# Gate and up projections with the weights as the stationary operand, and small loads moved in the load queue

## The chip, the cores and the metric

The kernel runs on one core of a Trainium2 chip. TensorE (PE in the profile) multiplies 128x128 tiles: a weight load (PEld) puts the stationary operand into the array, then a matmul streams the moving operand past it, up to 512 columns, and adds into a bank of PSUM. VectorE (DVE), ScalarE (ACT) and GpSimd (POOL) do the elementwise work, and SyncE (SP) issues nearly all DMAs, each of which moves 512 KB of weights from memory into a buffer on the chip. Each engine takes its instructions in the order in which the program lists them, and waits on semaphores where it needs another engine's result. The metric is the device time of one execution in microseconds (us), the median of several.

## The reference, cut to what matters

Two layers, each with a half-step SwiGLU FFN, a block of three token mixers and a second FFN. There are 256 tokens, the model's width is 1024 and the FFN's is 2816; everything is float32.

```python
def swiglu_ffn(h, w_gate, w_up, w_down):
    return (jax.nn.silu(h @ w_gate) * (h @ w_up)) @ w_down

for l in range(DEPTH):                                   # DEPTH = 2
    x = x + 0.5 * swiglu_ffn(rms_norm(x, ffn1_norm[l]), ffn1_w_gate[l], ffn1_w_up[l], ffn1_w_down[l])
    h = rms_norm(x, mix_norm[l])
    p = h @ w_in[l]                                      # 2320 columns, then attention, gMLP, linear attention
    ...
    x = x + (mixed @ w_out[l]).astype(x.dtype)
    x = x + 0.5 * swiglu_ffn(rms_norm(x, ffn2_norm[l]), ffn2_w_gate[l], ffn2_w_up[l], ffn2_w_down[l])
```

## The kernel before

**Three products for one.** A float32 operand is split into a high part (rounded to float32r, which TensorE takes in one pass) and a low part (the rest). A product is then high x high, high x low and low x high: `mm3` issues these three matmuls, and each has a weight load of its own.

**Weights.** All weights come in units of 128 x 1024 (512 KB). `Unit.split` loads one into a ring of 4 raw buffers (`load`, L166), casts it to the high part on ACT (`act`, L140, 128x1024) and subtracts that on DVE for the low part (`vec`, L155, two of 128x512). The high and low parts have rings of 10 buffers each.

**FFN.** The hidden width is cut into NJ = 11 blocks `j` of 256 columns. For each of the two token tiles t (128 tokens), `gate_up(j, t)` takes the transposed, normalized activations `hT[t]` as stationary operand and streams 512 columns of weights, 256 of gate and 256 of up, over eight slices kc of the model's width: 8 x 3 = 24 matmuls of 512 columns into a bank `gu`. ACT takes the silu of the gate half (scaled by `rstd[t]`, a number per token, which is a partition here) and DVE multiplies it by the up half. The result has tokens on the partitions, so `turn_act(j)` transposes it with four PE transposes (L123) into a bank `tr` and splits it into high and low parts (ACT cast, DVE subtraction). `down(j, t)` then uses it as stationary operand against the down weights, 12 matmuls of 512 columns into the banks `acc`. A block has 2 x 24 + 2 x 12 = 72 such matmuls. The second tile's `down` of the last two blocks is held back for `finish_b`, so that the first tile's residual and norm overlap with matmuls.

**Mixers.** `mix_phase` has five projections with the same `mm3` (four of 512 columns, one of 272), attention scores with float32r matmuls of 256 columns, many small matmuls, and an output projection. Its small parameters `col`, `row`, `wg` and `wsT` are loaded by SP (L166); `kgain` is a product of two columns of `col` on DVE.

**Order.** Every operation is first recorded in a `Plan` with an estimated cost. `issue()` simulates the engines with these costs and writes each engine's list, always taking the ready operation with the longest path to the end; matmuls marked bulk keep their order among themselves and give way to the others. `after=` adds a dependency for this planning alone. A load that depends on nothing is planned as soon as the load queue is free.

Of the kernel before, what the change touches and what calls it, by code (L numbers as in the profile page):

```python
# [17 lines left out]
P = 128  # L18
D = 1024
KC = D // P  # L20
# [20 lines left out]
class Plan:  # L41
# [72 lines left out]

    def mm(self, out, lhsT, rhs, start=True, stop=True, bulk=False, shared=False):
        n = rhs.free_size()
        cost = n / 2400.0 + 0.003 if lhsT.dtype == F32R else 4 * n / 2400.0 + 0.005
        return self.add("PE", cost, lambda: self.nc.tensor.matmul(out, lhsT, rhs, start=start, stop=stop,  # L118
                                                                  skip_group_check=shared),
                        [out], [lhsT, rhs], bulk)  # L120
# [40 lines left out]
    def pool(self, cost, call, writes, reads=()):  # L161
        return self.add("POOL", cost, call, writes, reads)

    def load(self, out, in_):
        nbytes = out.free_size() * out.partition_size() * 4
        return self.add("DMA", max(0.1, nbytes / 360e3), lambda: self.nc.sync.dma_start(out=out, in_=in_), [out], [])  # L166

    def load_small(self, out, in_):
        return self.add("ACT", 0.1, lambda: self.nc.scalar.dma_start(out=out, in_=in_), [out], [])
# [50 lines left out]
def hybrid_trunk(ctx: ExitStack, tc: tile.TileContext, x_in, norms, w_gu1, w_d1, w_in, w_out,  # L220
# [19 lines left out]
    for name in ("acc0", "acc1", "acc2", "acc3", "gu0", "gu1", "tr0", "tr1"):  # L240
        banks[name] = ps.tile([P, 512], F32, tag=name, name=name)
        pl.psum.add(banks[name].tensor.name)
    turns = {"gu": 0, "tr": 0}

    def bank(kind):
        if kind in turns:
            turns[kind] ^= 1
            return banks[f"{kind}{turns[kind]}"]
        return banks[kind]
# [11 lines left out]
    tri, upp, bdm = tile_("tri", P), tile_("upp", P), tile_("bdm", P)  # L261
    gcol = tile_("gcol", 3 * L, KC)
    xt = [tile_(f"x{t}", D) for t in range(2)]
    hT = [[tile_(f"h{t}{i}", KC, P, dtype=F32R) for i in range(2)] for t in range(2)]
    mix_a = [tile_(f"ma{i}", 2, 4, P, dtype=F32R) for i in range(2)]
    mix_b = [cut(hT[1][i], "p (t c) q -> p t c q", t=2) for i in range(2)]
    q_hl = tile_("q_hl", 8, 2, 64, dtype=F32R)
# [5 lines left out]
    flat = cut(E[1], "p h k q -> p (h k q)")  # L273
    acts = [flat[:, i * FB:(i + 1) * FB] for i in range(4)]
    gates_ = [flat[:, (4 + i) * FB:(5 + i) * FB] for i in range(2)]
    hg = Ring("hg", 2, 4, P)
    junk = cut(E[0], "p h k q -> p (h k q)").bitcast(BF16)[:, 0:D]
    raws = Ring("raw", RAW_BUFS, UW)
# [62 lines left out]
    pl.pool(0.5, lambda: make_identity(nc, ident), [ident])  # L341
    pl.vec("tensor_copy", out=ident_r, in_=ident)
    fill(mhalf, -0.5)
    pl.load_small(gcol, norms)
    for t in range(2):
        for n in range(2):
# [2 lines left out]

    def constants():  # L350
        fill(lrT, 1.0)
        for t in (wg, v_pad, kst, attnT, amask, bdm):
            fill(t, 0.0)
        select(amask[:, 0, :], [[1, P]], 0, -1, ALU.is_gt, NEG)
        select(amask[:, 1, :], [[-1, P]], 0, 1, ALU.is_ge, NEG)
        fill(tri, 1.0 / 16.0)
        fill(tri[0:64, 64:128], 0.0)
        select(tri, [[1, P]], 0, -1, ALU.is_ge, 0.0)
        fill(upp, 1.0 / 16.0)
        fill(upp[64:128, 0:64], 0.0)  # L360
        select(upp, [[-1, P]], 0, 1, ALU.is_gt, 0.0)
        fill(bdm[0:64, 0:64], 1.0)
        fill(bdm[64:128, 64:128], 1.0)


    rstd = [None, None]
    last_silu = [None]

    def rsqrt_mean(name, n, ssum, scale):
        v = small("v" + name, n)  # L370
# [36 lines left out]
    def ffn_phase(l, gu, dn):  # L407
        acc = [[banks["acc0"], banks["acc1"]], [banks["acc2"], banks["acc3"]]]
        g_units = [units_of(gu[l, j], UW, 4) for j in range(NJ)]
        d_units = [units_of(dn[l, j], UW, 2) for j in range(NJ)]  # L410
        act_tiles = {}
        aT = [[cut(mix_a[i][:, s], "p (t f) q -> p t f q", t=2) for i in range(2)] for s in range(2)] + [a_third]

        def gate_up(j, t):
            o = bank("gu")
            hi, lo = hT[t]
            for kc in range(KC):
                u = g_units[j][kc // 2]
                s = slice((kc % 2) * 512, (kc % 2) * 512 + 512)
                mm3(o, hi[:, kc, :], lo[:, kc, :], u.h[:, s], u.l[:, s], kc == 0, kc == KC - 1)  # L420
            sg, a = gates_[t], acts[2 * (j % 2) + t]
            pl.act(sg, o[:, 0:FB], AF.Silu, scale=rstd[t], extra=1.283 if j == 0 and t == 0 else 0.0)
            last_silu[0] = pl.ops[-1]
            pl.vec("scalar_tensor_tensor", out=a, in0=o[:, FB:2 * FB], scalar=rstd[t], in1=sg,
                   op0=ALU.mult, op1=ALU.mult)
            act_tiles[j, t] = a

        def turn_act(j):
            tr = cut(bank("tr"), "p (t f q) -> p t f q", t=2, f=2)
            for t in range(2):  # L430
                for f in range(2):
                    pl.turn(tr[:, t, f, :], act_tiles[j, t][:, f * P:(f + 1) * P], ident)
            split_psum(aT[j % 3][0], aT[j % 3][1], tr)

        def down(j, t):
            hi, lo = aT[j % 3]
            for f, n in ((0, 0), (1, 0), (0, 1), (1, 1)):
                u = d_units[j][f]
                s = slice(n * 512, (n + 1) * 512)
                mm3(acc[t][n], hi[:, t, f, :], lo[:, t, f, :], u.h[:, s], u.l[:, s],  # L440
                    j == 0 and f == 0, j == NJ - 1 and f == 1)

        for j in range(NJ):
            ready(g_units[j])
            gate_up(j, 0)
            if j > 0:
                turn_act(j - 1)
            gate_up(j, 1)
            if j > 0:
                ready(d_units[j - 1])  # L450
                down(j - 1, 0)
                if j < NJ - 2:
                    down(j - 1, 1)
                elif j == NJ - 1:
                    down(j - 2, 1)
        turn_act(NJ - 1)
        ready(d_units[NJ - 1])

        def finish_a():
            down(NJ - 1, 0)  # L460
            return acc[0]

        def finish_b():
            down(NJ - 2, 1)
            down(NJ - 1, 1)
            return acc[1]

        return finish_a, finish_b, 0.5


    def mix_phase(l):
        pl.load(col, pcol[l])
        pl.load(row, prow[l].partition_broadcast(P))
        pl.vec("tensor_tensor", out=kgain, in0=col[:, 0:1], in1=col[:, 1:2], op=ALU.mult)
        pl.load(wg[0:17], gla_wg[l])
        pl.load(wsT, sgu_wT[l])
        select(wsT, [[0, 4], [1, P]], 0, -1, ALU.is_ge, 0.0)

        off, i_units = 0, []
# [322 lines left out]
def _layout(inp):  # L802
    import numpy as np

    a = {k: np.ascontiguousarray(v) for k, v in inp.items()}

    def tiles(w):
        return np.ascontiguousarray(w)

    def gate_up(g, u):  # L810
        gu = np.stack([g.reshape(L, KC, P, NJ, FB), u.reshape(L, KC, P, NJ, FB)], axis=4)
        return tiles(gu.transpose(0, 3, 2, 1, 4, 5)).reshape(L, NJ, P, KC * 2 * FB)

    def down(w):
        return tiles(w.reshape(L, NJ, 2, P, D).transpose(0, 1, 3, 2, 4)).reshape(L, NJ, P, 2 * D)

    w = a["w_in"]
    aq = w[:, :, 0:512].reshape(L, D, 2, 4, 64).transpose(0, 1, 3, 2, 4).reshape(L, D, 512)
    kvl = np.concatenate([w[:, :, 512:768], w[:, :, 2304:2320]], axis=2)
    groups = [aq, kvl, w[:, :, 1280:1792], w[:, :, 1792:2304], w[:, :, 768:1280]]  # L820
    w_in = np.concatenate(
        [g.reshape(L, KC, P, g.shape[2]).transpose(0, 2, 1, 3).reshape(L, P, -1) for g in groups], axis=2)
    w = a["w_out"]
    att = w[:, 0:512].reshape(L, 2, 4, 64, D).transpose(0, 2, 1, 3, 4).reshape(L, 512, D)
    wo = np.concatenate([att, w[:, 768:1024], w[:, 512:768]], axis=1)
    w_out = wo.reshape(L, KC, P, D).transpose(0, 2, 1, 3).reshape(L, P, KC * D)
    norms = np.stack([a["ffn1_norm"], a["mix_norm"], a["ffn2_norm"]], axis=1)
    norms = norms.reshape(3 * L, KC, P).transpose(2, 0, 1)
    qg, kg = a["attn_q_norm"], a["attn_k_norm"]
    pcol = np.concatenate([np.concatenate([qg, qg], axis=1)[:, :, None], np.concatenate([kg, kg], axis=1)[:, :, None],  # L830
                           a["sgu_b"].transpose(0, 2, 1)], axis=2)
    sinks = a["attn_sinks"].reshape(L, 2, 4).transpose(0, 2, 1).reshape(L, 8)
    prow = np.concatenate([sinks, a["gla_out_norm"], a["sgu_v_norm"]], axis=1)
    wsT = a["sgu_w"].transpose(0, 3, 1, 2)
    wg = np.concatenate([a["gla_w_gate_up"], a["gla_b_gate"][:, None, :]], axis=1)
    return [
        ("x", a["x"].reshape(256, D)),
        ("norms", norms),
        ("w_gu1", gate_up(a["ffn1_w_gate"], a["ffn1_w_up"])),
        ("w_d1", down(a["ffn1_w_down"])),  # L840
        ("w_in", w_in),
        ("w_out", w_out),
        ("w_gu2", gate_up(a["ffn2_w_gate"], a["ffn2_w_up"])),
        ("w_d2", down(a["ffn2_w_down"])),
        ("pcol", pcol),
        ("prow", prow),
        ("sgu_wT", wsT),
        ("gla_wg", wg),
    ]
# [18 lines left out]
```

## Time and profile before

| | us |
|---|---|
| median of 3 runs (965.47 to 967.37) | 966.42 |
| the profiled execution: its time | 965.04 |
| the profiled execution: span from the first to the last instruction | 963.3 |

The granted TensorE clock is 1.000 on average over the span. PE is busy for 951.2 us of it, PEld for 779.5, DVE for 592.3, ACT for 479.1, POOL for 39.3. A matmul's end is modelled in the trace and matmuls overlap, so the rate at which PE works is read from the distance between their starts, or from the chain of waits, which lists a run of matmuls with their count and the time that they took together. Where the trace says `gu<-wh,h`, a matmul or weight load writes (or prepares) the bank `gu` from the high part of a weight and from `hT`.

### The profile page before, as it was taken

How to read it: one execution, taken by the hardware profiler on the slowest of the kernel's cores; microseconds unless marked ns; L12 is line 12 of the kernel's file. 1: busy time of each engine (PE TensorE's matmuls, PEld its weight loads, DVE VectorE, ACT ScalarE, POOL GpSimd, SP SyncE). 2: the span in 40 equal slices, each digit the busy share in tenths (PEclk: the TensorE clock that was granted, in tenths of full speed). 3: DMA queues.
4: the chain of work that ended last, by engine and by line, in shares of the span. 5: the costliest groups of instructions: out<-in, count | busy, mean ns of one | idle time of the engine just before them, and what ended most of it. 6: DMA issues, size and time to landing. Idle time of an engine off the chain costs nothing.

```text
span 963.3 us, 12361 instructions
## 1 busy us (share of the span) xinstructions
PE 951.2 (99%) x4484; PEld 779.5 (81%) x4484; DVE 592.3 (61%) x1115; ACT 479.1 (50%) x648; POOL 39.3 (4%) x52
## 2 busy tenths in 40 slices
PE   7999999999999999999999999999999999999998
PEld 5788888888788888888878888888887888888886
DVE  6765554498777455655486555455987775565551
ACT  6654544476566444545365444445666464454430
POOL 3000000020020000000010000000200100000000
PEclk9999999999999999999999999999999999999999
DMA  8866565366245565565466656563642556555531
GB/s 280 279 203 199 171 198 175 121 215 192 79 151 175 183 206 187 172 202 172 131 216 196 200 172 200 175 208 96 224 132 88 175 175 196 195 172 200 169 118 44
DMA packets 48626, 169.65 MB, mean 176 GB/s; under 512 B 5778, under 2 KB 7092, under 8 KB 48564
## 3 DMA queue, kind: packets, MB, share of 16 engines
q1 hardware_dynamic: 47844, 168.30, 53.5%
q8 instruction: 35, 0.57, 0.2%
q10 hardware_dynamic: 720, 0.55, 0.2%
q14 instruction: 27, 0.22, 0.1%
HBM read 167.78 MB, written 1.05 MB: 175 GB/s over the span
## 4 chain that ended last, share of the span: by engine, by line
PE 94%; DMA 3%; DVE 1%; ACT 1%; issue 0%; SPq 0%; DVEq 0%; ACTq 0%
PE gu L118 50%; PE acc L118 39%; PE tr L123 4%; DMA raw<-in_w_gu 2%; DMA raw<-in_w_d 1%; ACT wh L140 1%; DVE wl L155 1%; DMA raw<-in_w_in 1%; ACT h L140 0%; DVE hg L155 0%; ACT L142 0%; DVE h L155 0%; DVE e L155 0%; ACT e L142 0%; DVE qn L155 0%
## 5 line engine op out<-in xcount | busy, mean ns | idle before, releaser
L155 DVE TENSOR_TENSOR wl<-raw,wh 128x512 fp32r<-128x512 f32 (+2 forms) x636 | 408.8, 685 | 164.3 <-ACT wh L140 159.4
L118 PE MATMUL gu<-wh,h 128*128 128x512 f32 x1408 | 447.5, 394 | 2.4 <-ACT h L140 2.4
L140 ACT CAST wh<-raw 128x1024 fp32r<-128x1024 f32 (+2 forms) x318 | 327.7, 1045 | 174.1 <-PE acc L118 79.7
L118 PEld LDWEIGHTS gu<-wh,h 128*128 128x128 f32 x1408 | 261.4, 188 | 55.0 <-ACT h L140 2.8
L118 PE MATMUL gu<-wl,h 128*128 128x512 f32 x704 | 276.0, 392 | 0.0
L118 PE MATMUL acc<-wh,ma 128*128 128x512 f32 x576 | 188.5, 396 | 0.0
L118 PEld LDWEIGHTS gu<-wl,h 128*128 128x128 f32 x704 | 132.5, 188 | 28.1
L142 ACT ACTIVATE e<-gu,rn 128x256 f32<-128x256 f32 x88 | 41.8, 475 | 178.9 <-PE gu L118 178.9
L118 PEld LDWEIGHTS acc<-wh,ma 128*128 128x128 f32 x576 | 106.1, 188 | 20.6
L155 DVE SCALAR_TENSOR_TENSOR e<-gu,rn,e 128x256 f32<-128x256 f32 x88 | 42.3, 481 | 130.1 <-ACT e L142 130.0
L118 PE MATMUL acc<-wh,h 128*128 128x512 f32 (+1 forms) x384 | 120.2, 384 | 0.0
L118 PE MATMUL acc<-wl,ma 128*128 128x512 f32 x288 | 112.9, 392 | 0.0
L118 PEld LDWEIGHTS acc<-wh,h 128*128 128x128 f32 x384 | 69.3, 188 | 12.9 <-issue 2.0
L118 PE MATMUL acc<-wl,h 128*128 128x512 f32 (+1 forms) x192 | 73.8, 384 | 0.0
L118 PEld LDWEIGHTS acc<-wl,ma 128*128 128x128 f32 x288 | 54.1, 188 | 11.5
L118 PE MATMUL acc<-wh,q_hl 128*128 128x512 f32 x192 | 63.0, 395 | 0.0
L123 PE MATMUL tr<-ident,e 128*128 128x128 f32 x208 | 40.1, 272 | 1.7 <-DVE e L155 1.7
L118 PEld LDWEIGHTS acc<-wh,q_hl 128*128 128x128 f32 x192 | 35.5, 188 | 7.0
L118 PEld LDWEIGHTS acc<-wl,h 128*128 128x128 f32 x192 | 36.1, 188 | 6.0 <-issue 0.7
L123 PEld LDWEIGHTS tr<-ident,e 128*128 128x128 f32 x208 | 28.4, 139 | 14.6 <-DVE e L155 2.9
L140 ACT CAST ma<-tr 128x512 fp32r<-128x512 f32 x36 | 21.1, 587 | 37.5 <-PE tr L123 37.3
L118 PE MATMUL acc<-wl,q_hl 128*128 128x512 f32 x96 | 37.6, 391 | 0.0
(135 smaller groups left out, 463.3 us busy)
## 6 DMA issues: line engine op xcount, KB each, us to landing
raw<-in_w_gu SPq DMA_DIRECT2D x176, 512.0 KB, 4.4
raw<-in_w_d SPq DMA_DIRECT2D x88, 512.0 KB, 5.5
raw<-in_w_in SPq DMA_DIRECT2D x32, 512.0 KB, 4.4
raw<-in_w_out SPq DMA_DIRECT2D x16, 512.0 KB, 3.6
raw<-in_w_in SPq DMA_DIRECT2D x4, 408.0 KB, 3.1
x<-in_x SPq DMA_DIRECT2D x4, 256.0 KB, 6.0
raw<-in_w_in SPq DMA_DIRECT2D x2, 272.0 KB, 2.7
wsT<-in_sgu_wT SPq DMA_DIRECT2D x2, 256.0 KB, 3.4
```

Source lines behind the costliest of these rows:

```text
L118: return self.add("PE", cost, lambda: self.nc.tensor.matmul(out, lhsT, rhs, start=start, stop=stop, skip_group_check=shared), [out], [lhsT ...
L123: return self.add("PE", 0.056 if in_.dtype == F32R else 0.109, lambda: self.nc.tensor.transpose(out=out, in_=in_, identity=ident), [out], ...
L140: call = lambda: self.nc.scalar.copy(out=out, in_=in_)
L142: call = lambda: self.nc.scalar.activation(out=out, in_=in_, func=func, scale=scale, **kw)
L155: return self.add("DVE", cost, lambda: getattr(self.nc.vector, name)(**kw), writes, reads, after=after)
```

## The change

- The gate and up weights of all blocks but the first of each FFN are laid out on the host so that a unit holds, for one half b of a block (128 hidden columns) and for gate (i = 0) or up (i = 1), all eight slices of the model's width.
- `hT` becomes a view of one tile `hx`, in which a slice kc holds the high parts of both token tiles (256 columns) and then the low parts (256 columns).
- `gate_up_turned(j, b)` takes a 128x128 slice of weights as stationary operand. With the high part of the weights it streams all 512 columns of `hx[:, kc]` (8 matmuls of 512 columns: high x high into the left half of a bank, high x low into the right half); with the low part it streams the 256 columns of high parts (8 matmuls of 256 columns, into the right half). The eight of one width follow each other. Four banks are used in turn (`gu0`, `tr0`, `gu1`, `tr1`).
- The result has hidden columns on the partitions, so these blocks have no `turn_act`. For each unit ACT copies the right half of the bank and DVE adds the left half; for each half block DVE multiplies by `R`, ACT takes the silu, DVE multiplies gate and up, and ACT and DVE split the product into high and low parts.
- `R` holds `rstd` along the free axis on every partition. `row_scale` makes it once in an FFN: two diagonal matrices on DVE, two float32 matmuls of 128 columns with a matrix of ones, and a copy on ACT.
- The loads of `col`, `row`, `wg` and `wsT` are planned `after` the last bulk matmul of the gate and up part of block NJ - 5 of the FFN ahead, and `kgain` after its last silu. `wg` is zeroed once, at the beginning.
- Two costs of the plan change: a float32r matmul by 9 ns, and a DMA from 360 to 260 GB/s.

```diff
-        cost = n / 2400.0 + 0.003 if lhsT.dtype == F32R else 4 * n / 2400.0 + 0.005
+        cost = n / 2400.0 + 0.012 if lhsT.dtype == F32R else 4 * n / 2400.0 + 0.005
...
-        return self.add("DMA", max(0.1, nbytes / 360e3), lambda: self.nc.sync.dma_start(out=out, in_=in_), [out], [])
+        return self.add("DMA", max(0.1, nbytes / 260e3), lambda: self.nc.sync.dma_start(out=out, in_=in_), [out], [],
+                        after=after)
...
     def bank(kind):
+        if kind == "wide":
+            wide_turn[0] += 1
+            return banks[("gu0", "tr0", "gu1", "tr1")[wide_turn[0] % 4]]
...
-    hT = [[tile_(f"h{t}{i}", KC, P, dtype=F32R) for i in range(2)] for t in range(2)]
+    hx = tile_("hx", KC, 2, 2 * P, dtype=F32R)
+    hT = [[hx[:, :, i, t * P:(t + 1) * P] for i in range(2)] for t in range(2)]
+    ones, R = tile_("ones", P), tile_("R", 2 * P)
...
+        def row_scale():
+
+            b = banks["tr1"]
+            d = hg()
+            for t in range(2):
+                pl.vec("tensor_scalar", out=d[:, t, :], in0=ident, scalar1=rstd[t], scalar2=None, op0=ALU.mult)
+                pl.mm(b[:, t * P:(t + 1) * P], ones, d[:, t, :])
+            pl.act(R, b[:, 0:2 * P])
+
+        def gate_up_turned(j, b):
+
+
+            z = zs[z_turn[0] % 4]
+            z_turn[0] += 1
+            for i in range(2):
+                u, o = g_units[j][2 * b + i], bank("wide")
+
+                def high(start):
+                    for kc in range(KC):
+                        pl.mm(o, u.h[:, kc * P:(kc + 1) * P], hx[:, kc], start=start and kc == 0,
+                              stop=not start and kc == KC - 1, bulk=True, shared=True)
+
+                def low(start):
+                    for kc in range(KC):
+                        pl.mm(o[:, 256:512], u.l[:, kc * P:(kc + 1) * P], hx[:, kc, 0, :], start=start and kc == 0,
+                              stop=not start and kc == KC - 1, bulk=True, shared=True)
+
+                if i == 0:
+                    high(True)
+                    low(False)
+                else:
+                    low(True)
+                    high(False)
+                zi = z[:, i * 256:(i + 1) * 256]
+                pl.act(zi, o[:, 256:512])
+                pl.vec("tensor_tensor", out=zi, in0=o[:, 0:256], in1=zi, op=ALU.add)
+            z2 = cut(z, "p (i q) -> p i q", i=2)
+            pl.vec("tensor_tensor", out=z2, in0=z2, in1=R.unsqueeze(1).broadcast_to([P, 2, 256]), op=ALU.mult)
+            pl.act(z[:, 0:256], z[:, 0:256], AF.Silu)
+            last_silu[0] = pl.ops[-1]
+            a = z[:, 256:512]
+            pl.vec("tensor_tensor", out=a, in0=a, in1=z[:, 0:256], op=ALU.mult)
+            hi, lo = (x[:, :, b, :] for x in aT[j % 3])
+            split_psum(hi, lo, cut(a, "p (t q) -> p t q", t=2))
...
-        for j in range(NJ):
+        ready(g_units[0])
+        gate_up(0, 0)
+        gate_up(0, 1)
+        row_scale()
+        for j in range(1, NJ):
             ready(g_units[j])
-            gate_up(j, 0)
-            if j > 0:
-                turn_act(j - 1)
-            gate_up(j, 1)
-            if j > 0:
-                ready(d_units[j - 1])
-                down(j - 1, 0)
-                if j < NJ - 2:
-                    down(j - 1, 1)
-                elif j == NJ - 1:
-                    down(j - 2, 1)
-        turn_act(NJ - 1)
+            gate_up_turned(j, 0)
+            if j == 1:
+                turn_act(0)
+            gate_up_turned(j, 1)
+            if j == NJ - 5:
+                late_in_ffn[0] = pl.last_bulk
+            ready(d_units[j - 1])
+            down(j - 1, 0)
+            if j < NJ - 2:
+                down(j - 1, 1)
+            elif j == NJ - 1:
+                down(j - 2, 1)
...
-        pl.load(col, pcol[l])
-        pl.load(row, prow[l].partition_broadcast(P))
-        pl.vec("tensor_tensor", out=kgain, in0=col[:, 0:1], in1=col[:, 1:2], op=ALU.mult)
-        pl.load(wg[0:17], gla_wg[l])
-        pl.load(wsT, sgu_wT[l])
+        early = [late_in_ffn[0]]
+        pl.load(col, pcol[l], after=early)
+        pl.load(row, prow[l].partition_broadcast(P), after=early)
+        pl.vec("tensor_tensor", out=kgain, in0=col[:, 0:1], in1=col[:, 1:2], op=ALU.mult, after=[last_silu[0]])
+        pl.load(wg[0:17], gla_wg[l], after=early)
+        pl.load(wsT, sgu_wT[l], after=early)
```

## Rows read from the trace of the kernel before

**Rows 1.** The page's part 1: busy time, share of the span, instructions.
```profile
PE 951.2 (99%) x4484; PEld 779.5 (81%) x4484; DVE 592.3 (61%) x1115; ACT 479.1 (50%) x648; POOL 39.3 (4%) x52
```

**Rows 2.** The page's part 4: the chain that ended last, by engine.
```profile
PE 94%; DMA 3%; DVE 1%; ACT 1%; issue 0%; SPq 0%; DVEq 0%; ACTq 0%
```

**Rows 3.** The chain in order, one FFN block: start us, us, what, count.
```profile
57.89 7.26 PE gu L118 x32
65.14 0.22 PE tr L123 x2
65.36 3.66 PE gu L118 x16
69.02 2.50 PE acc L118 x11
71.52 0.22 PE tr L123 x2
71.74 3.00 PE acc L118 x13
```

**Rows 4.** Stretches: length, busy us (count) PE, PEld, DVE, ACT, POOL; clock, DMA share, GB/s.
```profile
57.89:74.74 16.85, 16.85 (x77) 13.86 (x77) 9.24 (x15) 7.63 (x10) 0.00 (x0) 1.00 0.61 206
...
211.00:215.40 4.40, 4.40 (x38) 4.40 (x36) 4.40 (x9) 3.37 (x5) 0.43 (x1) 1.00 0.78 260
```

**Rows 5.** The chain around the start's weight loads.
```profile
18.43 4.94 DMA raw<-in_w_d
...
29.96 5.11 DMA raw<-in_w_d
...
37.37 0.44 PE tr L123 x2
```

**Rows 6.** A stretch at the start, columns as in rows 4.
```profile
20.00:40.00 20.00, 18.95 (x87) 15.07 (x86) 16.71 (x28) 12.94 (x16) 1.07 (x1) 1.00 0.86 286
```

**Rows 7.** The chain in the projections; the 80 are 42 of 512, 38 of 272.
```profile
201.35 14.31 PE acc L118 x80
```

**Rows 8.** The chain in the mixers: float32 `gu` of 256; score `gu` of 256 among projections.
```profile
224.82 0.43 PE gu L118 x2
...
236.40 0.70 PE acc L118 x3
237.09 0.47 PE gu L118 x4
```

**Rows 9.** Groups by line, 211.0 to 215.4 us, weight loads: busy us, mean ns, idle.
```profile
L118 PEld LDWEIGHTS acc<-wh,h 128*128 128x128 f32 x24 | 3.8, 188 | 0.0
```

**Rows 10.** Groups by line and shape, DVE and ACT: busy us, mean ns.
```profile
L155 DVE TENSOR_TENSOR wl<-raw,wh 128x512 fp32r<-128x512 f32 x624 | 402.8, 688 | 164.3 <-ACT wh L140 159.4
L155 DVE SCALAR_TENSOR_TENSOR e<-gu,rn,e 128x256 f32<-128x256 f32 x88 | 42.3, 481 | 130.1 <-ACT e L142 130.0
...
L140 ACT CAST wh<-raw 128x1024 fp32r<-128x1024 f32 x312 | 323.2, 1050 | 173.9 <-PE acc L118 79.7 <-PE gu L118 68.9 <-DMA raw<-in_w_gu 9.8
L142 ACT ACTIVATE e<-gu,rn 128x256 f32<-128x256 f32 x88 | 41.8, 475 | 178.9 <-PE gu L118 178.9
L140 ACT CAST ma<-tr 128x512 fp32r<-128x512 f32 x36 | 21.1, 587 | 37.5 <-PE tr L123 37.3
```

**Rows 11.** SP's DMA issues and a DVE instruction near 16 to 20 us.
```profile
15.81 0.32 SPq L166 DMA_DIRECT2D wg<-in_gla_wg  x1
...
17.04 0.43 SPq L166 DMA_DIRECT2D wsT<-in_sgu_wT  x1
...
20.14 0.16 DVE L155 TENSOR_TENSOR kgain<-col 128x1 f32<-128x1 f32 x1 [0.95 <-DMA col<-in_pcol]
```

**Rows 12.** DMA issues: count, KB each, median us to landing.
```profile
wsT<-in_sgu_wT SPq DMA_DIRECT2D x2, 256.0 KB, 3.4
...
row<-in_prow SPq DMA_DIRECT2D x2, 164.0 KB, 4.9
```

More of the change, by code (lines that the diff above doesn't have):

```diff
@@ L162, in pool, with load @@
         return self.add("POOL", cost, call, writes, reads)
-    def load(self, out, in_):
+    def load(self, out, in_, after=()):
         nbytes = out.free_size() * out.partition_size() * 4
-        return self.add("DMA", max(0.1, nbytes / 360e3), lambda: self.nc.sync.dma_start(out=out, in_=in_), [out], [])
+        return self.add("DMA", max(0.1, nbytes / 260e3), lambda: self.nc.sync.dma_start(out=out, in_=in_), [out], [],
+                        after=after)
     def load_small(self, out, in_):
@@ L243, in hybrid_trunk @@
     turns = {"gu": 0, "tr": 0}
+    wide_turn = [0]
     def bank(kind):
+        if kind == "wide":
+            wide_turn[0] += 1
+            return banks[("gu0", "tr0", "gu1", "tr1")[wide_turn[0] % 4]]
         if kind in turns:
@@ L275, in hybrid_trunk @@
     gates_ = [flat[:, (4 + i) * FB:(5 + i) * FB] for i in range(2)]
+    zs = [flat[:, i * 512:(i + 1) * 512] for i in range(4)]
     hg = Ring("hg", 2, 4, P)
@@ L343, in hybrid_trunk @@
     fill(mhalf, -0.5)
+    fill(ones, 1.0)
+    fill(wg, 0.0)
     pl.load_small(gcol, norms)
@@ L351, in constants @@
         fill(lrT, 1.0)
-        for t in (wg, v_pad, kst, attnT, amask, bdm):
+        for t in (v_pad, kst, attnT, amask, bdm):
             fill(t, 0.0)
@@ L366, in hybrid_trunk @@
     rstd = [None, None]
-    last_silu = [None]
+    last_silu, late_in_ffn = [None], [None]
     def rsqrt_mean(name, n, ssum, scale):
@@ L409, in ffn_phase @@
         g_units = [units_of(gu[l, j], UW, 4) for j in range(NJ)]
+        z_turn = [2]
         d_units = [units_of(dn[l, j], UW, 2) for j in range(NJ)]
@@ L426, in gate_up @@
             act_tiles[j, t] = a
+        def row_scale():
[35 more added lines that the diff above has]
+            split_psum(hi, lo, cut(a, "p (t q) -> p t q", t=2))
         def turn_act(j):
-            tr = cut(bank("tr"), "p (t f q) -> p t f q", t=2, f=2)
+            tr = cut(banks["tr0"], "p (t f q) -> p t f q", t=2, f=2)
             for t in range(2):
@@ L811, in gate_up @@
         gu = np.stack([g.reshape(L, KC, P, NJ, FB), u.reshape(L, KC, P, NJ, FB)], axis=4)
-        return tiles(gu.transpose(0, 3, 2, 1, 4, 5)).reshape(L, NJ, P, KC * 2 * FB)
+        first = gu[:, :, :, :1].transpose(0, 3, 2, 1, 4, 5).reshape(L, 1, P, KC * 2 * FB)
+        rest = gu[:, :, :, 1:].reshape(L, KC, P, NJ - 1, 2, 2, P).transpose(0, 3, 2, 5, 4, 1, 6)
+        return np.concatenate([first, rest.reshape(L, NJ - 1, P, KC * 2 * FB)], axis=1)
     def down(w):
```

## Prediction

> **What bounds the kernel now.** I read the page first. Part 1 shows PE busy for 951.2 of 963.3 us, and the chain of waits is 94% PE [rows 1, 2]. That could be 94% of work or of modelled ends, so the next view is the chain in order of time. There a block of the FFN repeats with a period of 16.85 us (from 57.89 to 74.74), and every piece of it is PE [rows 3]. A run of 32 matmuls takes 7.26 us, so a matmul of 512 columns has a price of 0.2269 us. The block's 72 such matmuls make 16.34 us, and what is left, 0.51 us, is the price of its four transposes with the unevenness that they leave in the runs behind them. In the same block DVE is busy for 9.24 and ACT for 7.63 us, and the DMAs carry 206 GB/s [rows 4], where the start of the kernel shows 286 [rows 6]. So in the 40 blocks that are changed (ten in each of four FFNs) nothing but PE's list sets the time. The one stretch with another bound is the start: between 18 and 37 us the chain passes through loads of weights [rows 5], and from 20 to 40 us PE is idle for 1.05 us, with the DMAs at 0.86 of their time [rows 6].
>
> **The change part by part.** Sums are made against the profiled execution, 965.04 us (its span of 963.3 and 1.7 around it), which is 1.4 us under the median of 966.42.
>
> *Gate and up.* A block now has 48 matmuls of 512 columns. After it, a unit has 8 of 512 and 8 of 256, and four units make 32 and 32. The columns are the same, 24,576; the matmuls are 16 more. So all hangs on the price of a matmul of 256 columns with a weight load of its own. The FFN shows none, but two places do. In the projections 80 matmuls take 14.31 us; the 42 of 512 make 9.53 of it, and the 38 of 272 cost 0.1258 each [rows 7]. Between 272 and 512 columns that is 0.421 ns per column and 11 ns per matmul, so 256 columns come to 0.1191. In the attention scores four of 256 take 0.47, 0.1175 each; with both changes of width around them (1.16 us from 236.40 to 237.56, less three of 0.2269) it is 0.1198 [rows 8]. I take 0.119, and as bounds 0.1175 and 0.1258. Per block 32 x 0.119 - 16 x 0.2269 = +0.178; 40 blocks **+7.1 us** (+5.2 to +15.8).
>
> *Transposes.* 160 of the 176 in the four FFNs go (the first block of each keeps its four): 40 x 0.51 = **-20.4 us**. Their ACT casts and DVE subtractions become others, below.
>
> *Row scale.* Two float32 matmuls of 128 columns in each FFN. A pair of transposes costs 0.255 (above), two float32 matmuls of 256 columns 0.43 [rows 8]. I take the first, whose shape they have: **+1.0 us** (to +1.7). Behind them on PE waits the second block's gate and up; their own input, `rstd`, is what the first block's silus need anyhow, 10.9 us of matmuls (48 x 0.2269) earlier in the list.
>
> *Weight loads.* They speak against the change above all. There are 40 x 12 more (64 instead of 52 outside `down`), each recorded with 188 ns [rows 9], longer than the 119 that a narrow matmul may take. But among the 272-wide matmuls 36 loads of 188 ns stand in 4.40 us [rows 4, 9]: 6.8 us of loads, so they overlap each other. And the 11 ns beside the columns are the same at 272 and 512 columns; a load that held the matmul up would cost the narrow one more. The Trainium skill says otherwise (TensorE: Matmul & The Clock Gate, The mechanism): a weight load overlaps a matmul in flight only when it goes to other row groups of the array. By that rule each matmul here, all on 128 rows, would pay its load after its columns; by the same page's LDWEIGHTS section, which gives 107 ns for 128 columns, a wide one would take 320 ns and a narrow one 213 (an estimate), and gate and up would come to 40 x (32 x 0.213 - 16 x 0.320) = +68 us where I have +7.1. The trace doesn't agree: 227 ns a wide one.
>
> *Elementwise work,* costed at nothing on the cover of PE. Per block DVE loses two products (0.481 each) and a subtraction (0.69); it gains four additions, two products and two subtractions of 256 columns, each at most 0.481, and two products with `R` of 512 at 0.688 [rows 10]: 9.24 - 1.65 + 5.22 = 12.8 us. ACT loses two silus (0.475) and a cast (0.587) and gains eight instructions of 256 at most 0.475: 7.63 - 1.54 + 3.8 = 9.9 us. Both fit in the 16.5 us that PE needs. A bank is used again after three other units, 3 x (8 x 0.2269 + 8 x 0.119) = 8.3 us, and is free after one copy and one addition, 0.96. Where the cover is thin is the end of an FFN. From the last matmul of gate and up to the last part that `down(10)` needs, copy, addition, `R`, silu, product, cast and subtraction follow each other: 3 x 0.475 + 3 x 0.481 + 0.688 = 3.56 us. In between stand `down(9, 0)` and `down(8, 1)`, 24 x 0.2269 = 5.45 us. So 1.9 us are left for queueing behind weight splits. I take nothing; the bound is in the second rival.
>
> *Demand for weights.* Before, a block's four units are all needed within its first 24 matmuls (5.45 us); after, one every 2.77 us. With 206 of 286 GB/s this can only ease waits.
>
> *Small loads and `kgain`.* In the first layer the four loads are issued from 15.81 to 17.04 us [rows 11], ahead of the load of down weights that the chain passes through at 18.43 [rows 5]; two of them alone carry 420 KB [rows 12], 1.5 us at 286 GB/s. DVE then stands 0.95 us for `kgain`, with seven weight splits behind it [rows 11]. After the change both come in the middle of the FFN, where the DMAs have room: the weight loads behind them on SP come 1.5 us later, against a block's period of 16.5. `after` is no semaphore, so SP waits for nothing new there. This can give back no more than PE's idle 1.05 us in the stretch: I take **-0.7 us** (0 to -1.1). In the second layer they leave the mixers, where no piece of the chain waits for them: nothing. Zeroing `wg` earlier is POOL work ahead of nothing that PE waits for.
>
> *The plan's costs.* They change no instruction, only the order. All of PE's idle time is 12 us [rows 1], so a new order in the mixers can take or bring a stall like the one at the start: 0, with 1 us to either side.
>
> *Sum:* +7.1 - 20.4 + 1.0 - 0.7 = -13.0 us: 952.0 for a profiled execution and **953.4** for the median. The bounds together make -16.3 (950.1) and -1.8 (964.6), the latter nearly all from the price of the narrow matmul.
>
> **The rivals.**
> 1. *Slower: weight loads pace the narrow matmuls.* If two loads in a row can't overlap under matmuls this short, 1,280 narrow ones take 188 ns instead of 119: +88 us, 1,041. It decides from 129 ns on, where 13.0 us are used up (0.119 + 13.0/1,280). For it: the load's 188 ns, and PEld busy without a break at 272 columns [rows 4]. Against it: those matmuls' 126 ns, and the scores' 117.5. 5%. (The skill's rule above is a stronger form of this, with 61 us on the forecast, 1,014, an estimate; the trace's wide matmuls leave it at most 1% of these 5.)
> 2. *The end of an FFN waits for its activations.* If each of the three ACT steps comes behind a cast (1.05) and each of the three DVE steps behind a subtraction (0.688) [rows 10], the chain takes 3.56 + 5.2 = 8.8 us, 3.3 more than its cover. The last FFN has no weights to split behind it, so it is three times at most 3.3: up to 963.3, and half of the queueing gives 955.6. For it: DVE at 78% of a block. Against it: the plan puts the longest path first, and casts fill 6.3 of 16.5 us of ACT. 14%, at 956 to 963.
> 3. *Narrow ones cost what the 272-wide ones do,* 0.1258, since something other than the columns sets their pace: +8.7 us, 962.1. Against it are the scores. 6%.
> 4. *The start gives nothing:* 954.1, inside the forecast's own range.
>
> **How the numbers follow.** 72% for the forecast, whose own range is 950 to 957.5; 3% for less than 949, from a better order. 949 to 961 holds the forecast, most of rival 2, and leaves out rivals 1 and 3 and what is below. A change of under 0.2% (1.9 us) is about what can't be told from none: that is 964.5 to 968.4, which the worst of rival 2 and 3 with the upper bounds reach, 4%. Slower is rival 1, 5%. The rest, 91%, is faster.
>
> **What would show it.** A block of the chain with no `tr` piece and a period of 16.85 - 0.33 = 16.52 us; runs of 16 narrow matmuls in 1.90 us; DVE busy some 12.5 us in a block; no `acc` run near the end of an FFN broken by a wait for `z` or the split; from 20 to 40 us less PE idle. The prediction is wrong if the narrow runs take over 2.1 us, or if PE is idle for more than 1 us ahead of `down(10, 0)`.

## The result and the profile after

The changed kernel takes 952.68 us (median of 4 runs, 952.32 to 952.94), beside 966.47 for the kernel before: a ratio of 0.9859, 95% interval 0.9843 to 0.9875. Forecast were 953.4 us and a range of 949 to 961. The profiled execution went from 965.04 to 952.68, its span from 963.3 to 950.8; the other runs of the kernel before were up to 2.3 us longer than its profiled one.

The page of the changed kernel, parts 1 and 4, to be read against [rows 1, 2]:

```profile
PE 940.5 (99%) x4980; PEld 800.1 (84%) x4980; DVE 693.4 (73%) x1403; ACT 525.8 (55%) x852; POOL 40.2 (4%) x53
...
PE 99%; POOL 0%; ACT 0%; DVE 0%; issue 0%; DVEq 0%; POOLq 0%
```

There are 496 more matmuls and as many more weight loads, and still less time. (16 more in each of the 40 blocks make 640; 160 transposes fewer and 16 of the row scale, whose eight float32 matmuls the profile lists twice each, make 496.) DVE is at 73% instead of 61%, and the 3% of DMA have left the chain.

One FFN block in the chain of waits of the changed kernel, against [rows 3]; a piece of 16 is a unit, 8 wide and 8 narrow matmuls:

```profile
40.12 2.77 PE tr L118 x16
42.88 2.80 PE gu L118 x16
45.68 2.77 PE tr L118 x16
48.45 2.80 PE gu L118 x16
51.25 5.44 PE acc L118 x24
56.69 1.36 PE tr L118 x6
```

The period is 56.69 - 40.12 = 16.57 us; it was 16.85, and 16.52 was forecast. No transposes are left (the `tr` pieces are matmuls of L118 now; the banks `tr` have become two of the four wide ones). Gate and up take 11.14 us, where 48 wide matmuls took 10.89.

The start and two later blocks as stretches, columns as in [rows 4]:

```profile
20.00:40.00 20.00, 20.00 (x107) 17.16 (x106) 17.51 (x33) 14.97 (x23) 0.00 (x0) 1.00 0.74 251
...
122.85:139.43 16.58, 16.58 (x90) 14.35 (x89) 12.09 (x22) 8.74 (x15) 1.17 (x1) 1.00 0.59 201
139.43:156.01 16.58, 16.58 (x90) 14.35 (x89) 11.72 (x22) 8.82 (x15) 0.00 (x0) 1.00 0.56 187
```

PE has no idle time in any of them; against [rows 6] the 1.05 us at the start are gone. In these two blocks DVE works 12 us (12.5 were forecast) and ACT 8.8 (9.9 at most), inside PE's 16.58, and the DMAs bring 187 to 201 GB/s. The first blocks after the start do more, since weights are split ahead there: from 39.95 to 56.53 us DVE works 13.9 and ACT 10.4, still inside it.

**Where the time went.** The blocks come in the same order in both kernels, so the distance between the first matmul of one stretch and that of the next can be compared. Worked out from the matmuls' starts in the trace (us); the last five columns are experiments, below:

```
                                   before   after  costs_  loads_  old_   old_   turned_
                                                   alone   alone   loads  costs  alone
span start to FFN 1's third block   40.86   39.96  40.74   40.78   40.30  39.85   39.69
  of it, first block                14.62   15.23  15.76   14.72   15.73  15.75   15.35
  of it, second block               18.55   17.07  17.13   18.57   17.07  17.05   17.04
blocks 3 to 11 of an FFN (x4)      149.00  146.44 149.00  149.00  146.44 146.44  146.44
first block of a later FFN          12.08   12.27  12.08   12.08   12.27  12.28   12.28
second block of the third FFN       17.95   17.21  17.10   17.55   18.07  17.03   17.04
mixers, first layer                 99.23   98.81  98.81   99.17   98.77  99.79   99.40
mixers, second layer                99.49   98.83  98.81   99.56   99.36  99.23   99.27
span                               963.32  950.85 961.23  962.84  953.07 951.94  952.64
```

(The third FFN is the first of the second layer. Second blocks elsewhere take 17.13 us before and 17.05 after; first blocks are the lowest of three.) Of the 12.5 us between the spans, the blocks gave 4 x (2.56 + 0.08) = 10.6 and the two mixers 1.1. Beside the blocks' 0.08, the start gave 0.8 and the second block of the third FFN 0.7. The first blocks took back some 0.2 in each later FFN, 0.6 in all: the row scale came in, and two of the transposes left for the second block. In the first FFN this is within the start's 0.8.

The start's 0.8 is a sum of two things. The second block lost a stall of 1.4 us (18.55, where 17.13 is usual before). The first block's length depends on the execution: the eight runs whose first block has the changed kernel's order take 15.16 to 15.73 us for it. The wide matmuls of the first block start 0.43 us apart at first and 0.23 later; the change comes at 11.7 us in the kernel before and at 13.9 in costs_alone. So the second block is the better measure of a stall.

### The profile page after: what moved, and what is told of

Same layout as the page of the kernel before. It is cut to its first block, busy times and chain, and to the rows that moved or that the text cites. A ratio compares the mean times of both kernels' runs of the same rounds, so it can differ in the third digit from the quotient of the medians.

```text
span 950.8 us, 13681 instructions
## 1 busy us (share of the span) xinstructions
PE 940.5 (99%) x4980; PEld 800.1 (84%) x4980; DVE 693.4 (73%) x1403; ACT 525.8 (55%) x852; POOL 40.2 (4%) x53
## 3 DMA queue, kind: packets, MB, share of 16 engines
HBM read 167.78 MB, written 1.05 MB: 178 GB/s over the span
## 4 chain that ended last, share of the span: by engine, by line
PE 99%; POOL 0%; ACT 0%; DVE 0%; issue 0%; DVEq 0%; POOLq 0%
PE acc L118 41%; PE gu L118 31%; PE tr L118 23%; PE tr L123 3%; ACT wh L140 0%; DVE hg L155 0%; POOL kst L347 0%; ACT hx L140 0%; DVE x L155 0%; DVEq L927 0%; POOL upp L347 0%; POOL ident masks.py:199 0%; POOL tri L343 0%; POOL amask L347 0%; POOL wg L347 0%
## 5 line engine op out<-in xcount | busy, mean ns | idle before, releaser
L118 PE MATMUL acc<-wh,ma 128*128 128x512 f32 x576 | 184.0, 390 | 0.0
L118 PE MATMUL gu<-hx,wh 128*128 128x512 f32 x640 | 160.8, 392 | 0.0
L118 PE MATMUL tr<-hx,wh 128*128 128x512 f32 x640 | 158.4, 389 | 0.0
L118 PEld LDWEIGHTS tr<-hx,wh 128*128 128x128 f32 x640 | 120.0, 188 | 24.9
L118 PEld LDWEIGHTS gu<-hx,wh 128*128 128x128 f32 x640 | 115.0, 189 | 20.4
L118 PEld LDWEIGHTS acc<-wh,ma 128*128 128x128 f32 x576 | 107.7, 188 | 21.9
L118 PE MATMUL acc<-wh,hx 128*128 128x512 f32 (+1 forms) x384 | 118.2, 383 | 0.0
L118 PE MATMUL acc<-wl,ma 128*128 128x512 f32 x288 | 112.5, 390 | 0.0
L118 PEld LDWEIGHTS tr<-hx,wl 128*128 128x128 f32 x640 | 87.3, 190 | 6.3
L118 PE MATMUL gu<-hx,wl 128*128 128x256 f32 x640 | 89.9, 283 | 0.0
L118 PE MATMUL tr<-hx,wl 128*128 128x256 f32 x640 | 89.2, 282 | 0.0
L118 PEld LDWEIGHTS gu<-hx,wl 128*128 128x128 f32 x640 | 82.5, 192 | 0.1
L118 PEld LDWEIGHTS acc<-wh,hx 128*128 128x128 f32 x384 | 69.1, 188 | 13.1 <-issue 2.3
L118 PE MATMUL acc<-wl,hx 128*128 128x512 f32 (+1 forms) x192 | 72.9, 380 | 0.0
L118 PEld LDWEIGHTS acc<-wl,ma 128*128 128x128 f32 x288 | 54.1, 188 | 11.3
L118 PE MATMUL acc<-wh,q_hl 128*128 128x512 f32 x192 | 61.7, 389 | 0.0
```

## The experiments

**Three parts, one at a time.** First the plan's costs alone, on the kernel before:

```diff
-        cost = n / 2400.0 + 0.003 if lhsT.dtype == F32R else 4 * n / 2400.0 + 0.005
+        cost = n / 2400.0 + 0.012 if lhsT.dtype == F32R else 4 * n / 2400.0 + 0.005
...
-        return self.add("DMA", max(0.1, nbytes / 360e3), ...
+        return self.add("DMA", max(0.1, nbytes / 260e3), ...
```

> The kernel before with the two costs of the plan alone (float32r matmul + 9 ns, DMA 260 GB/s). The mixers are 0.4 and 0.7 us shorter in the changed kernel although no instruction of theirs changed. Theory: that is the new order that these costs give, so here the mixers lose about 1.1 us and the median is 965.4. Rival: the mixers' gain comes from their small loads being on the chip already; then this run is at 966.5, within 0.3.

Measured: 962.47 us, with 965.51 for the kernel before beside it, ratio 0.9958 (0.9941 to 0.9974). That is 2.9 us below the theory's number. Both mixers take 98.81 us, as in the changed kernel, so their 1.1 us are the order that the costs give. The third FFN's stall is gone too, 0.85 us. And so is the first FFN's, with the transposes still there: its second block takes 17.13 us, and PE has no idle time in the start's stretch, against [rows 6]:

```profile
20.00:40.00 20.00, 20.00 (x93) 16.30 (x92) 15.69 (x28) 13.50 (x17) 0.00 (x0) 1.00 0.72 238
```

The third block starts at 40.74 all the same, because the first block was 1.1 us longer in this run. The rest of the difference in medians is not in this pair of profiled executions, which differ by 2.1 us.

Then the small loads and `kgain` alone (with the early zeroing of `wg`), on the kernel before:

```diff
-        pl.load(col, pcol[l])
+        pl.load(col, pcol[l], after=early)
...
-        pl.vec("tensor_tensor", out=kgain, in0=col[:, 0:1], in1=col[:, 1:2], op=ALU.mult)
+        pl.vec("tensor_tensor", out=kgain, in0=col[:, 0:1], in1=col[:, 1:2], op=ALU.mult, after=[last_silu[0]])
```

> The kernel before with the small loads and kgain planned in the FFN, and the early zeroing of wg, alone. Theory of the prediction: it gives back part of PE's idle 1.05 us between 20 and 40 us and nothing else, so 965.8 (965.4 to 966.5). Rival: the start gains from the smoother demand for weights of the turned blocks and not from the moved loads; then 966.5, within 0.3, and PE's idle time from 20 to 40 us stays at 1 us.

Measured: 964.58 us, again beside 965.51, ratio 0.9995 (0.9983 to 1.0008), no change that can be told. The start shows why; its stretch in this run, against [rows 6]:

```profile
20.00:40.00 20.00, 18.97 (x86) 15.05 (x85) 15.24 (x26) 12.07 (x15) 0.00 (x0) 1.00 0.79 262
```

The four loads are no longer there (the one of `row` is issued at 123.2 us), the DMAs' share fell from 0.86 to 0.79, and PE is idle for 1.03 us where it was 1.05. FFN 1's second block takes 18.57 us instead of 18.55.

The reverse, the changed kernel without the moved loads (`early = []`, and no `after` for `kgain`):

> The changed kernel with its small loads and kgain planned as before. Theory of the prediction: the start loses what the moved loads gave, 0.7 us: 953.4. Rival (smoother demand gave it): 952.7, within 0.3.

Measured: 952.98 us, ratio 0.9872 (0.9853 to 0.9890). The median speaks for the rival. Its profiled execution was its longest (955.03); it shows a stall in the second block of the third FFN (18.07 us, where 17.05 is usual) and longer second mixers (99.36). As the other executions were up to 2.2 us shorter, these probably belong to that execution; they weren't traced, and whether the moved loads make such executions rarer stays open.

The changed kernel with the old costs:

> The changed kernel with the old costs in the plan (float32r matmul + 3 ns, DMA 360 GB/s). Theory: the mixers' 1.1 us come from the costs and go again: 953.8. Rival: the order doesn't matter: 952.7, within 0.3.

Measured: 954.04 us, ratio 0.9879 (0.9858 to 0.9900). The mixers go back to 99.79 and 99.23, and little else in the table changes: the theory holds.

The turned blocks alone, the kernel before with neither of the two other parts:

> The kernel before with the turned blocks alone: the small loads planned as before and the old costs of the plan. The stretches of the trace so far say: blocks -10.6 us, row scale +0.7, the stall in the first FFN's second block gone (-1.4), mixers as before. So a profiled execution comes to 953.5 to 954.5, and the two other parts of the change are worth 1 to 2 us on top. Rival: turned blocks without the other parts stall at the start as before, 955.5.

Measured: 953.58 us, ratio 0.9866 (0.9849 to 0.9884), with a third block that starts at 39.69 us although the small loads are where they were, and with no idle time of PE in the start's stretch:

```profile
20.00:40.00 20.00, 20.00 (x108) 17.20 (x107) 16.57 (x30) 12.74 (x19) 0.96 (x1) 1.00 0.80 264
```

FFN 1's second block takes 17.04 us. So the turned blocks alone take away the first FFN's stall, as the costs alone do, and they make nearly the whole result: 12.3 us in the medians of this pair. (The profiled execution is 1.8 us longer than the changed kernel's: 1.0 in the mixers, 1.2 behind the last matmul, where this execution took 4.9 us and the changed kernel's 3.7, less 0.4 at the start and in the third FFN.)

**What paces a narrow matmul.** The changed kernel with 128 columns in place of 256 in the low part; the second token tile's low x high product is left out:

```diff
-                        pl.mm(o[:, 256:512], u.l[:, kc * P:(kc + 1) * P], hx[:, kc, 0, :], start=start and kc == 0,
+                        pl.mm(o[:, 256:384], u.l[:, kc * P:(kc + 1) * P], hx[:, kc, 0, 0:P], start=start and kc == 0,
```

> The changed kernel with the low part of the weights streaming 128 columns in place of 256 (the second token tile's low x high product is left out): 1,280 matmuls have the same weight loads and half the columns. Theory of the prediction, columns at 0.417 ns and some 11 ns per matmul: 0.1195 falls to 0.066, so 68 us less, 884. Rival 1 of the prediction (weight loads pace the narrow matmuls): nothing changes, 952.7. A floor between the two, as the float32r transposes of 128 columns in the mixers suggest with 80 to 85 ns between their starts, gives 0.083 and 906.

Measured: 945.01 us (one execution). Half of the columns of 1,280 matmuls gave 7.7 us, not 68. The theory of the prediction falls for narrower matmuls. Two explanations were left: a floor per weight load, or half pace for float32r below 256 columns, which 192 columns tell apart (`hx[:, kc, 0, 0:192]`):

> The changed kernel with the low part of the weights streaming 192 columns in place of 256 (low x high for the second half of tile 1 is left out). The run with 128 columns gained 7.7 us where the columns' pace gave 68, some 113 ns per matmul: either a floor that goes with each matmul's weight load (then 192 columns cost 113 to 116 ns too and the time is about 946 to 949), or a float32r matmul of under 256 columns streams at half the pace (128 columns 107 ns and 6 more; then 192 columns cost 166 ns and the time rises by 60 us to 1,012). Columns at 0.417 ns and 11 more, the prediction's reading, give 91 ns and 916.

Measured: 942.06 us, below the 946 to 949 of a floor and far from the other two. It is a floor: 192 columns cost no more than 128. (They even take 3 us less; that lies in the wide matmuls behind the narrow ones, and why isn't shown.) Chain of waits of the run with 128 columns, gate and up of one block:

```profile
105.32 2.65 PE tr L118 x16
107.98 2.81 PE gu L118 x16
110.78 2.67 PE tr L118 x16
113.45 2.81 PE gu L118 x16
```

And of the run with 192:

```profile
105.33 2.68 PE tr L118 x16
108.02 2.74 PE gu L118 x16
110.76 2.68 PE tr L118 x16
113.44 2.74 PE gu L118 x16
```

Less 32 wide matmuls at 0.2269, a narrow one comes to (10.94 - 7.26) / 32 = 0.115 us with 128 columns, (10.84 - 7.26) / 32 = 0.112 with 192, and in the changed kernel (11.14 - 7.26) / 32 = 0.121 with 256, changes of width included. The weight loads in the timeline of the run with 192 columns stand at the floor:

```profile
107.77 0.97 PEld L118 LDWEIGHTS gu<-hx,wl 128*128 128x128 f32 x8
```

Eight loads, each recorded with 192 ns, take 0.97 us from the first start to the last end: (0.97 - 0.19) / 7 = 0.111 us from one to the next. Only the distance shows the pace, not the recorded length. That it is the load which sets this floor isn't shown: each narrow matmul has one load, and no run parts the two. Nor is it a floor of every load of 128 x 128. The mixers have float32r transposes of 128 columns, whose loads stand closer (kernel before, weight loads in the timeline):

```profile
215.54 0.73 PEld L123 LDWEIGHTS tr<-ident_r,q_hl 128*128 128x128 f32 x8
```

With some 0.14 recorded for each that is (0.73 - 0.14) / 7 = 0.084 us.

To the other side, 384 columns (the first tile's low x low product is added):

> The changed kernel with the low part streaming 384 columns in place of 256 (it adds the low x low product of the first token tile, so it is work on top). Columns at 0.417 ns beside a fixed 11 to 13 ns: 173 ns in place of 119.5, +68 us, 1,021. If the 119.5 of 256 columns is set by the weight load, part of the 128 columns is free: a load floor of 113 ns is already under the 256 columns' own 107 + 11, so hardly any, and the time is 1,013 to 1,021.

Measured: 1,024.82 us, 3.8 over the expected 1,021. In its chain the four units of a block take 3.23, 3.24, 3.23 and 3.24 us, two of them here:

```profile
115.45 3.23 PE tr L118 x16
118.68 3.24 PE gu L118 x16
```

(12.94 - 7.26) / 32 = 0.1775, changes of width included, so 128 columns more cost 56 ns, 0.44 ns per column: from 256 up the columns pace, as in the rows of before.

**Widths in turn.** The changed kernel with a wide and a narrow matmul for each slice:

```diff
+                for kc in range(KC):
+                    pl.mm(o, u.h[:, kc * P:(kc + 1) * P], hx[:, kc], start=kc == 0,
+                          stop=False, bulk=True, shared=True)
+                    pl.mm(o[:, 256:512], u.l[:, kc * P:(kc + 1) * P], hx[:, kc, 0, :], start=False,
+                          stop=kc == KC - 1, bulk=True, shared=True)
```

> The changed kernel with the two widths alternating, wide and narrow for each slice of the model's width: a block has 32 changes from narrow to wide in place of 2. The changed kernel's run of 8 wide matmuls takes 1.841 us behind narrow ones and 1.814 otherwise, 0.027 more. Theory 1, each change costs that: 30 x 40 x 0.027 = +32 us, 985. Theory 2, it costs what the attention scores show for a change there and back, 7 ns: +8 us, 961. Theory 3, width makes no difference by its order: 952.7.

Measured: 960.28 us. Its chain, the last two units of a block and the `down` behind them:

```profile
112.70 2.83 PE tr L118 x16
115.53 2.82 PE gu L118 x16
118.35 5.50 PE acc L118 x24
```

Blocks 3 to 11 take 148.42 us instead of 146.44, 0.22 per block for 30 more changes: 7 ns each, which is near theory 2 (1.16 us less three wide ones and the scores' 0.47 leave 9 ns [rows 8]). "One width together" is worth 7.6 us by this one execution, over half of the change's gain.

**Fewer changes still.** The two units of a half block share their order: both high parts, then both low parts, and the other way round for the second half:

```diff
+            for i in range(2):
+                (high if b == 0 else low)(i, True)
+            for i in range(2):
+                (low if b == 0 else high)(i, False)
```

> The changed kernel with the matmuls of one width of gate and up together: 16 wide and 16 narrow for the first half block, 16 narrow and 16 wide for the second, so one change from narrow to wide per block in place of two. If a change costs 0.027: 40 x 0.027 = 1.1 us less, 951.6. Rival: the units' high and low parts are wanted in pairs now and two banks are open at once, so that PE waits for weight splits, or the 0.027 isn't of the change: 952.7 or more.

Measured: 951.92 us, ratio 0.9858 (0.9838 to 0.9878), which can't be told from the changed kernel's 0.9859. Its chain, a block's gate and up:

```profile
106.31 1.81 PE tr L118 x8
108.12 1.81 PE gu L118 x8
109.94 0.95 PE tr L118 x8
110.89 0.96 PE gu L118 x8
111.85 0.96 PE tr L118 x8
112.81 0.96 PE gu L118 x8
113.77 1.84 PE tr L118 x8
115.61 1.81 PE gu L118 x8
```

One run of wide matmuls takes 1.84 in place of 1.81 where there were two, and 32 narrow ones take 3.83, 0.1197 each. Blocks 3 to 11 take 146.26 instead of 146.44: 0.7 us over four FFNs, there in the trace and too small for the timing.

**The cover at the end of an FFN.** `down(9, 0)` and `down(8, 1)` ahead of the last half block:

```diff
+            if j == NJ - 1:
+                ready(d_units[j - 1])
+                down(j - 1, 0)
+                down(j - 2, 1)
+                gate_up_turned(j, 1)
+                continue
```

> The changed kernel with the 24 matmuls of down(9, 0) and down(8, 1) ahead of the last half block of gate and up of each FFN, so that nothing stands between it and down(10, 0). PE then waits in the open for the chain that the prediction put at 3.56 us. It needs the first cast after 3.08 us and has 3 matmuls (0.68) on the other half first: 2.4 us per FFN, +9.6 us, 962, and up to 5.2 us of queueing in each of three FFNs, 978 at most. Rival 2 of the prediction (the chain is as long as its cover of 5.45 us): 4 x 4.8 = +19 us or more, 972 and up.

Measured: 975.30 us. The last FFN shows the chain bare (chain of waits):

```profile
957.76 0.38 ACT e L140
...
958.16 0.43 DVE e L155
...
958.62 0.70 DVE e L155
...
959.35 0.42 ACT e L142
...
959.80 0.43 DVE e L155
...
960.25 0.41 ACT ma L140
...
960.71 9.18 PE acc L118 x33
```

From 957.68, where the chain leaves PE, to 960.66 it took 2.98 us to the first cast's end (3.08 in the prediction). Then the 33 matmuls cost 9.18 instead of 7.49 us. The same is seen better in the first FFN, where PE is idle for 4.02 us until 191.08 (stretches, columns as in [rows 4]):

```profile
185.00:190.00 5.00, 2.06 (x10) 1.35 (x8) 3.15 (x7) 3.11 (x5) 0.00 (x0) 1.00 0.43 122
190.00:195.00 5.00, 3.92 (x13) 3.04 (x14) 2.06 (x5) 1.02 (x2) 0.00 (x0) 0.73 0.54 177
```

The granted clock falls to 0.73 on average in the stretch in which PE goes on: a part of it went at the lower level of 1.2 GHz, the rest at 2.4. Here are that part and the like one of the last FFN, both with 0.50:

```profile
192.34:195.75 3.41, 3.41 (x11) 2.72 (x10) 1.31 (x3) 0.74 (x1) 0.00 (x0) 0.50 0.23 93
...
960.40:963.70 3.30, 2.99 (x7) 2.41 (x8) 1.18 (x3) 0.26 (x1) 0.00 (x0) 0.50 0.02 5
```

The stretch from `down(10, 0)` on is 6.0, 6.1, 6.6 and, in the last FFN, 4.0 us longer than in the changed kernel, 22.6 in all. PE's idle time makes 4.02 + 3.00 + 3.77 + 2.37 = 13.2 of it, and most of the rest is the lower clock, at which PE worked for some 17.8 us. So the idle time speaks for the theory and against rival 2: the bare chain costs the 2.4 us that were expected, and no FFN reaches the 4.8 of idle time that rival 2 needs, though the chain in the first FFN holds an ACT table load of 1.28 us. That the total also lies inside the theory's 962 to 978 is luck, since the theory allowed for queueing there and not for the clock.

## Why the prediction was right, step by step

**Gate and up: right in kind, under-sized.** Forecast was +0.178 us per block with 0.119 a matmul, and +7.1 in all; measured is 11.14 - 10.89 = +0.25, some +10. A narrow matmul takes 0.1197, as the grouped run shows (16 of them 1.91, where 1.90 was said), and twice in a block the wide run behind narrow ones takes 0.03 longer. The bound from the 272-wide ones (+15.8) held.

**Transposes: as forecast.** 0.51 us a block are gone. With the term above that makes 0.27 per block (16.85 to 16.58) where 0.33 was said: 10.6 us instead of 13.3.

**Row scale: under-sized.** The first block of a later FFN grew by only 0.19 us (12.08 to 12.27), but it also lost two transposes, 0.255 by the prediction's price (ten pieces of L123 stood in it before, eight after). So the row scale costs some 0.45, where 0.25 (1.0 / 4) was said, 1.8 in all, a little over the bound of 1.7. The reading behind it was wrong: the two pieces of 0.43 us in [rows 8] are one float32 matmul of 256 columns, which the profile lists twice. The two matmuls of the row scale make four pieces as well:

```profile
300.88 0.60 PE L118 MATMUL tr<-hg,ones 128*128 128x128 f32 x4
```

**Weight loads: the conclusion right, its reason incomplete.** They overlap and don't cost 188 ns, as said. But the step "the 11 ns beside the columns are the same at 272 and 512 columns; a load that held the matmul up would cost the narrow one more" can't see a floor that lies below 272 columns. There is one, at 112 ns for a load and its matmul; the 256-column matmuls stand 8 ns above it. Rival 1's price was wrong, since it took a load's recorded length for its pace; whether its mechanism, the load, sets the floor isn't shown. The Trainium skill (TensorE: Matmul & The Clock Gate, LDWEIGHTS) has 107 ns for a load of 128 columns whatever its rows; the measured 111 to 112 agree nearly, the 84 of the transposes don't. The Trainium skill's rule on row groups (TensorE: Matmul & The Clock Gate, The mechanism), weighed in the prediction, does not agree here: a wide matmul with its load takes 227 ns.

**Small loads and `kgain`: the failed step.** "Ahead of the load of down weights that the chain passes through" was a matter of neighbourhood, not of cause: with them gone PE is idle for 1.03 us, and FFN 1's second block takes 18.57 us as before. The start gained its 0.9 us (0.7 forecast) all the same, so this term is right by luck. The block's stall goes with the turned blocks alone (17.04), the loads unmoved. It also goes with the plan's costs alone (17.13), where the transposes and the demand for weights are as before. Either is enough. So the demand for weights (a unit every 2.77 us instead of four within 5.45), which was costed at nothing, isn't shown to be the cause. In both runs with the stall PE waited for the input of transposes [rows 5]; what brings that input in time stays open.

**The plan's costs: missed.** They were put at 0 with 1 us to either side; they are worth 1.1 us in the mixers, in the changed kernel and on their own, and on their own they also take away the two stalls, of the first and the third FFN.

**The sum: partly luck.** The misses nearly cancel: 2.5 us less from the blocks and the row scale together (9.8 for 12.3), 1.1 more from the mixers and 0.9 more from the start and the third FFN's stall. So the profiled executions differ by 12.4 us, where 13.0 were forecast. The forecast's median also held 1.4 us by which the median of the kernel before exceeds its profiled execution. The changed kernel has none of them (both are 952.68), which outweighs the 0.6 and puts the result 0.7 below the forecast. Why its executions lie closer together isn't shown.

**The end of an FFN: cover held.** In the changed kernel's first FFN the last gate and up matmuls end near 181.2 us. ACT and DVE in the timeline:

```profile
181.21 0.37 ACT L140 COPY e<-gu 128x256 f32<-128x256 f32 x1 [2.03 <-PE gu L118]
182.80 0.42 ACT L142 ACTIVATE e<-e 128x256 f32<-128x256 f32 x1 [1.22 <-DVE e L155]
183.24 1.28 ACT L613 ACT_TABLE_LOAD   x1
184.53 0.41 ACT L140 CAST ma<-e 128x256 fp32r<-128x256 f32 x1
...
184.97 0.42 DVE L155 TENSOR_TENSOR ma<-e,ma 128x256 fp32r<-128x256 f32 x1 [1.22 <-ACT ma L140]
```

And PE in the chain of waits:

```profile
178.32 2.80 PE gu L118 x16
181.12 8.62 PE acc L118 x38
```

The chain takes 185.39 - 181.21 = 4.18 us where 3.56 were worked out. No weight split stands in it, as the plan puts the longest path first, but an ACT table load of 1.28 us for the mixers does, which the prediction overlooked. The cast is done at 184.94; the 24 covering matmuls and three more last until about 187.2. So 2.3 us are left, and PE's run of 38 matmuls goes on at 0.2268 each. In the other three FFNs no two starts of matmuls there lie more than 0.32 us apart. Rival 2 didn't come.

## What to carry to other kernels

In a stretch that PE bounds alone, the list of matmuls with a price per width, read from the distance between starts in runs of the same width, gives the time; price each change of width too (7 ns here when widths alternate) and keep equal ones together. Take a price only within the range of sizes that the trace shows: below it a floor, here 112 ns for a load and its matmul, may already set the pace. Look whether a record is a whole instruction: a float32 matmul stands twice in the profile. And a transfer that stands ahead of a late one in the queue is not thereby its cause: take it out alone before counting its time as a gain. When one part alone removes a stall, try the other parts alone too: here two of them do.

## What the runs showed of the hardware

- In runs of narrow float32r matmuls, each with a weight load of 128 x 128, loads follow each other at 111 to 112 ns at best, though each is recorded with 188 to 192 ns: with 128 and with 192 columns a matmul costs about that, with 256 some 120, with 384 some 177. The loads of float32r transposes of 128 columns follow at 84 ns.
- A wide matmul behind narrow ones costs more for a while: eight of them 1.84 us in place of 1.81; in strict alternation a change there and back costs 7 ns.
- A float32 matmul is listed twice by the profile: one of 256 columns takes 0.43 us as two pieces.
- After 4.02 us without work PE went on at 191.08 us, and from 192.34 to 195.75 the granted clock was 0.50, the lower level of 1.2 GHz; in the last FFN, after 2.37 us without work, 33 matmuls took 9.18 us in place of 7.49. So a stall of PE cost more than its own length.
